# Folding the square sums of x on VectorE, and a new place for loads and fill work, in one layer of a gated encoder

## The chip, the cores and the metric

The kernel runs on one core of a Trainium2 chip. Five engines work side by side, each through its own list of instructions in order: TensorE (PE, with its weight loads as PEld), VectorE (DVE), ScalarE (ACT), GpSimd (POOL) and SyncE (SP), which issues all DMA transfers here. They wait for each other through semaphores. The metric is the device time of one launch in microseconds (us), the median of the runs shown. Everything is float32 in and out.

## What is computed

One encoder layer is applied to two requests, a prompt of 1024 tokens and a sample of 512, with the same weights. Cut to what matters:

```
def encoder_layer(x, mem, ...):
    h = rms_norm(x, ln_pre)
    z = h @ w_in                                  # 1024 -> 6400 columns
    (pool_in, pool_gate, q, k, v, attn_gate, xq, x_gate, merge_logits) = split(z)
    pool_out = multiscale_pool(pool_in, w_pool, pool_scale)
    q = apply_rope(rms_norm(q, q_norm));  k = apply_rope(rms_norm(k, k_norm))
    attn_out = self_attention(q, k, v)            # 8 heads of 64, 2 groups of k and v
    cross_out = cross_attention(xq, rms_norm(mem, ln_mem), w_mem_kv)   # 4 heads of 128, 256 memory tokens
    branches = (pool_out * silu(pool_gate), attn_out * silu(attn_gate), cross_out * silu(x_gate))
    gates = sigmoid(merge_logits + b_merge)
    merged = sum(gates[n] * (branches[n] @ w_branch[n]) for n in range(3))
    return x + rms_norm(merged @ w_out, ln_post)
```

`rms_norm` divides each token by the root of its mean square, so before h exists the squares of all 1024 features of a token must be summed.

## The kernel before

Every matrix product keeps float32 accuracy with three products of a cheaper type: each operand is split into a high and a low part (`split`, lines 171 to 173: ACT copies the high part, DVE subtracts it from the value for the low part), and `mm3` (line 139) issues high times high, high times low and low times high. Tiles hold 128 partitions by 512, 1024 or 2048 elements. Activations lie transposed, features on partitions and tokens along the row, in blocks of 512 tokens (`BLK`).

The program runs through these parts:

- `mem_phase` (line 655) projects the memory tokens of both requests: four chunks of keys (`mk`, 24 matmuls each), then four weight tiles of values (`mv`, 96 matmuls together). It also needs the mean squares of the memory tokens. It is given the generator `others` and steps it with `next(others, None)`.
- `others` is `long_h` (line 235): it loads the prompt's x as four tiles of 1 MB (`q[i][j]`, feature half i, token block j), sums the squares, scales x to h and forms the seven sums and differences that a fast 2x2 block multiplication needs (`put`, `difference`).
- Mean squares: `squares` (line 206) squares a 128x2048 tile on ACT and hands back its four pieces of 512. `mean_squares` (line 198) sums over the partitions on PE, by matmuls of each 128x128 piece with two columns of ones, 4 token tiles by as many pieces as it is given. ACT copies the result, `rstd_of` takes the power -0.5 on POOL, and `spread` (line 212) puts the row on all partitions: a diagonal on DVE, then one PE product with ones.
- `products` (line 313) multiplies h of the prompt with the weights, pair after pair, seven block products of 12 matmuls for each; `plain` (line 388) does it for the sample, 24 matmuls a weight tile. A generator of tails (`kv_tail`, `q_tail`, `pool_tail`) is stepped along.
- Then `stream` (line 807) runs a list of units: 64 of self attention of the prompt, 8 of cross attention, 32 of self attention of the sample, 4 of cross attention. Each unit has three steps, `scores`, `turn` (transposes of the probabilities on PE, split by ACT and DVE) and `values`; `turn` comes `LAG`=2 units behind `scores` and `values` another `VLAG`=2 behind. `weave` (line 108) counts the PE cost of these steps and after each of them adds steps of a generator `fill` until `SHARE` of that cost is used up. The fill is the rest of the sample's input products and then `branches(0)`, the branch projections of the prompt's first token block (`merge`, 288 matmuls).
- `block` (line 886) runs what is left: `branches` and `out_phase` block by block.

The order of each engine's list is then set by a scheduler from this order of emission, from the dependencies through tile buffers (`M` has 14 buffers of 2048, `HU` 8 of 512, `RAW` 3 weight tiles) and from priorities (`high_priority`). Each engine, SP too, takes its list strictly in order.

Of the kernel before, what the change touches and what calls it, by code (L numbers as in the profile page):

```python
# [19 lines left out]
D = 1024  # L20
KC = D // P
BLK = 512
# [39 lines left out]
def encoder_kernel(ctx: ExitStack, tc, wt, xs, xts, mt, cols, rows, rope, edge, ys):  # L62
# [64 lines left out]
    def chain(*gs):  # L127
        for g in gs:
            yield from g
# [75 lines left out]

    def squares(x):

        sq = M(F32)
        act.activation(sq[:], x, AF.Square, scale=D ** -0.5)
        return [sq[:, c * BLK:(c + 1) * BLK] for c in range(4)]  # L210

    def spread(r, out=None):

# [21 lines left out]
    def long_h(xt, h):  # L235

        h += [[None] * 4 for _ in range(7)]
        xv = xt.rearrange("p (k t) -> p k t", k=KC)
        q = [[M(F32) for _ in range(2)] for _ in range(2)]
        for j in range(2):  # L240
            for i in range(2):
                load(q[i][j][:].rearrange("p (c n) -> p c n", c=4), xv[:, i * 4:i * 4 + 4, j * BLK:(j + 1) * BLK])
                yield
        r, sp = S(16), []
        for j in range(2):
            rj = r[:, j * TT:(j + 1) * TT]
            mean_squares(squares(q[0][j][:]) + squares(q[1][j][:]), rj)
            rstd_of(rj)
            sp.append(spread(rj))
        b11, b12, b21, b22 = [[q[i][j][:, :D], q[i][j][:, D:]] for i in range(2) for j in range(2)]  # L250

        def scaled(i, j):
            for c in range(4):
                x = q[i][j][:, c * BLK:(c + 1) * BLK]
                v.scalar_tensor_tensor(x, x, colt[:, i * 4 + c:i * 4 + c + 1], sp[j], op0=ALU.mult, op1=ALU.mult)

        def put(k, x):
            for c in range(2):
                parts_of(h[k], 2 * c, x[c])

        def difference(out, a, b):
            for c in range(2):
                v.tensor_tensor(out[c], a[c], b[c], op=ALU.subtract)

        scaled(0, 0)
        put(0, b11)
        scaled(1, 0)
        put(1, b21)
        scaled(0, 1)
        scaled(1, 1)  # L270
        t3, t4 = (U(), U()), (U(), U())
        difference(t3, b22, b12)
        difference(b12, b12, b11)
        difference(b11, b22, b12)
        put(2, b11)
        put(3, b12)
        put(4, t3)
        put(5, b22)
        difference(t4, b21, b11)
        put(6, t4)  # L280
# [374 lines left out]
    def mem_phase(mkd, mvd, others):  # L655
# [7 lines left out]
        for i in range(4):  # L663
            x = raw[i // 2][:, i % 2 * D:(i % 2 + 1) * D]
            hi, lo = sb.tile([P, 1024], F32R, tag="kt", bufs=4, name=nm("mh")), U(F32R)
            for k in range(2):
                s = slice(k * BLK, (k + 1) * BLK)
                g = colt[:, 8 + 2 * i + k:9 + 2 * i + k]
                act.activation(hi[:, s], x[:, s], AF.Copy, scale=g)
                v.scalar_tensor_tensor(lo[:, s], x[:, s], g, hi[:, s].bitcast(F32), op0=ALU.mult, op1=ALU.subtract)  # L670
                mh.append(hi[:, s])
                ml.append(lo[:, s])
        yield
        m = list(zip(mh, ml))
        r, sp = S(16), HU()

        def rstd():
            mean_squares(squares(raw[0][:]) + squares(raw[1][:]), r[:, :TT])
            rstd_of(r[:, :TT])
            spread(r[:, :TT], sp[:])  # L680

        for c in range(4):
            b, w = B(), ws.pop(0) if ws else weights("mk", c)
            for k in range(KC):
                mm3(b[:], w(slice(k * P, (k + 1) * P)), m[k], k == 0, k == KC - 1)
            if c == 0:
                rstd()
            next(others, None)
            yield
            t, hi, lo = HU(), HU(F32R), HU(F32R)  # L690
            with tc.high_priority(EVAC):
                v.tensor_tensor(t[:], b[:], sp[:], op=ALU.mult)
                split(hi[:], lo[:], t[:])
            for g in range(2):
                for s, x in enumerate((hi, lo)):
                    o = s * D + c * NMEM
                    nc.sync.dma_start(mkd[g][:, o:o + NMEM], x[:, g * NMEM:(g + 1) * NMEM].bitcast(F32))
# [34 lines left out]
    def attention(b, sc, kt, vt, L):  # L732
# [4 lines left out]
        units = [(jp, hd, j) for jp in range(TT // 2) for hd in range(NH) for j in range(2)]  # L737
        state = {}

        def scores(i):  # L740
            jp, hd, j = units[i]
            g = hd // (NH // NG)
            if hd == 0 and j == 0:
                t = M()
                for x in range(2):
                    load(t[:, x * D:(x + 1) * D].bitcast(F32), qd[b * TT + jp * 2 + x][:])
                state["q", jp] = t
            q = state["q", jp][:, j * D + hd * P:j * D + (hd + 1) * P]
            a = A()
            for n in range(L // 512):  # L750
                ns = slice(n * 512, n * 512 + 512)
                mm(a[:, ns], q, kt[g][0][:, ns], start=True, stop=False)
                mm(a[:, ns], q, kt[g][1][:, ns], start=False, stop=True)
            mx, sm, rc = S(1), S(1), S(1)
            with tc.high_priority(PMAX):
                v.reduce_max(mx[:], a[:, :L], axis=AX.X, negate=True)  # L756
                p = U()
                act.activation(p[:, :L], a[:, :L], AF.Exp, bias=mx[:], accum_out=sm[:])  # L758
            v.reciprocal(rc[:], sm[:])  # L759
            pool.tensor_scalar(p[:, :L], p[:, :L], rc[:], 1.0, op0=ALU.mult, op1=ALU.mult)  # L760
            state[i] = p
# [40 lines left out]
                pool.tensor_tensor(ot[:, :256], ot[:, :256], gt[:, :256], op=ALU.mult)  # L802
                nc.sync.dma_start(out[c][:, cs], ot[:, :256])

        return [(scores, turn, values, i) for i in range(len(units))]

    def stream(units):
        n = len(units)
        for i in range(n + LAG + VLAG):
            for k, lag in enumerate((0, LAG, LAG + VLAG)):  # L810
                if 0 <= i - lag < n:
                    units[i - lag][k](units[i - lag][3])
                    yield

    def cross(b, sc, mkd, mvd):
# [2 lines left out]
        xqd, gd, out = sc["xq"], sc["x_gate"], sc["br2"]  # L818
        state = {}

        def scores(c):
            xf, xq = HU(), U(F32R)
            load(xf[:], xqd[c][:, bs])
            qh, ql = xq[:, 0:BLK], xq[:, BLK:2 * BLK]
# [2 lines left out]
            if c == 0:  # L827
                for k, src in (("mk", mkd), ("mv", mvd)):
                    t = M()
                    load(t[:].bitcast(F32), src[:])  # L830
                    state[k] = [t[:, i * D:(i + 1) * D] for i in range(2)]
            mk = state["mk"]
            a = A()
            ms_ = slice(c * NMEM, (c + 1) * NMEM)
            for t in range(TT):
# [36 lines left out]
        return [(scores, turn, values, c) for c in range(NXH)]  # L872

    def branch_parts(field, bs):
        t = from_scratch(field, bs)
# [139 lines left out]
    scs, kts, vts, pairs, bg, _, drained = group(0)  # L1015
    run(plain(pairs[0], hs, bg))
    merged = []
    fill = chain(drained(plain(pairs[1], hs, bg)), branches(0, sc, merged))
# [4 lines left out]
    run(fill)  # L1023
    run(block(1, 0, sc, False, merged))
    run(block(1, 1, sc, False))
    run(block(0, 0, scs, True))
# [1 line left out]

LAG, VLAG, SHARE, LOOK, WAIT = 2, 2, 0.9, 1, 6

AHEAD, EVAC, PMAX, PTURN, LATER = 120, 200, 150, 150, 200

# [89 lines left out]
```

## Time and profile before

| | us |
|---|---|
| median of 3 runs (1556.06 to 1563.41) | 1559.63 |
| the profiled execution, its own time | 1562.16 |
| its span on the core | 1559.9 |
| PE busy in the span | 1501.1 (96%) |
| DVE, ACT, POOL busy | 970.6 (62%), 711.3 (46%), 271.7 (17%) |

A window row of the profile gives, for a stretch of the span, each engine's busy time with its number of instructions, then the clock granted to TensorE (1.00 is full), the share of the DMA engines in use and GB/s. A timeline row gives start, duration, engine, line, operation, output and inputs by their names (buffer numbers left out), shape and count, and in brackets how long the engine had waited and for what. A chain row gives start, length and what stood on the chain of work that ended last.

### The profile page before, as it was taken

To read this page: it belongs to the slowest core of one execution; us is meant where nothing else is said; L and a number is where in the kernel's file an instruction comes from. 1 tells how busy PE (TensorE), PEld (TensorE's weight loads), DVE (VectorE), ACT (ScalarE), POOL (GpSimd) and SP (SyncE) were. 2 spreads that over 40 slices of the span, in tenths; PEclk is the share of its full clock that TensorE was granted. 3 is DMA by queue.
4 is the path that set the end of the run, shared out by engine and by line. 5 is a ranking of instruction groups with operands and counts; after the bars stand their busy time and mean duration, and the time that the engine had idled before them with its cause. 6 is when DMAs were issued, how large, how long until landed. Compare 5 with 4: busy or idle time off the path is not lost.

```text
span 1559.9 us, 19916 instructions
## 1 busy us (share of the span) xinstructions
PE 1501.1 (96%) x7408; PEld 1245.8 (80%) x7408; DVE 970.6 (62%) x1250; ACT 711.3 (46%) x1097; POOL 271.7 (17%) x286
## 2 busy tenths in 40 slices
PE   7979999999999999999999999999799889999998
PEld 5867888888888888887888888888586678888887
DVE  3278668574746765565666666666577674674764
ACT  3334435454433545443555555556445453333322
POOL 0000011110000000210222222223313350150141
PEclk8779999999999999999999999999899899999999
DMA  6421224333331443254232323225734564864942
GB/s 225 135 82 54 100 71 139 103 130 107 98 122 56 157 141 115 83 165 139 85 116 75 102 74 116 75 84 191 256 129 136 174 211 137 296 228 135 334 165 81
DMA packets 88176, 211.40 MB, mean 136 GB/s; under 512 B 9872, under 2 KB 19216, under 8 KB 87312
## 3 DMA queue, kind: packets, MB, share of 16 engines
q1 hardware_dynamic: 88080, 210.14, 40.3%
q8 instruction: 58, 0.95, 0.2%
q14 instruction: 38, 0.31, 0.1%
HBM read 155.57 MB, written 54.53 MB: 135 GB/s over the span
## 4 chain that ended last, share of the span: by engine, by line
PE 87%; issue 3%; DVE 3%; ACT 3%; DMA 2%; POOL 0%; SPq 0%; DVEq 0%; POOLq 0%; ACTq 0%
PE B L133 68%; PE A L133 14%; PE A L137 5%; DVE wlo L169 1%; ACT med L172 1%; PE B L137 1%; ACT whi L172 1%; ACT u L843 1%; DMA hu<-x_gate 0%; DVE med L169 0%; DMA hu<-merge 0%; ACT u L758 0%; DMA med<-q 0%; DMA hu<-xq 0%; DMA hu<-wt 0%
## 5 line engine op out<-in xcount | busy, mean ns | idle before, releaser
L133 PE MATMUL B<-med,whi 128*128 128x512 f32 x2776 | 874.7, 395 | 11.3 <-ACT med L172 10.6
L133 PEld LDWEIGHTS B<-med,whi 128*128 128x128 f32 x2776 | 516.7, 189 | 117.8 <-ACT med L172 12.5
L133 PE MATMUL B<-med,wlo 128*128 128x512 f32 x1388 | 546.6, 394 | 6.7 <-DVE wlo L169 6.7
L169 DVE TENSOR_TENSOR wlo<-raw,whi 128x1024 fp32r<-128x1024 f32 (+1 forms) x168 | 212.9, 1267 | 169.1 <-ACT whi L172 161.0
L133 PEld LDWEIGHTS B<-med,wlo 128*128 128x128 f32 x1388 | 263.0, 189 | 64.1 <-DVE wlo L169 8.2
L172 ACT ACTIVATE whi<-raw 128x1024 fp32r<-128x1024 f32 (+1 forms) x168 | 167.4, 996 | 305.3 <-PE B L133 191.6
L172 ACT ACTIVATE med<-A 128x1024 fp32r<-128x1024 f32 (+1 forms) x108 | 97.0, 898 | 143.4 <-PE A L137 143.0
L760 POOL TENSOR_SCALAR u<-u,s 128x1024 f32<-128x1024 f32 (+1 forms) x96 | 94.3, 982 | 339.1 <-DVE s L759 305.1
L169 DVE TENSOR_TENSOR med<-A,med 128x1024 fp32r<-128x1024 f32 (+1 forms) x109 | 115.5, 1060 | 49.0 <-ACT med L172 47.9
L192 POOL TENSOR_SCALAR s<-s 128x16 f32<-128x16 f32 (+3 forms) x17 | 5.3, 311 | 712.3 <-DVE s L551 330.0
L756 DVE TENSOR_REDUCE s<-A 128x1 f32<-128x1024 f32 (+1 forms) x96 | 100.0, 1041 | 38.8 <-PE A L133 25.7
L758 ACT ACTIVATE u<-A,s 128x1024 f32<-128x1024 f32 (+1 forms) x96 | 93.2, 971 | 47.5 <-DVE s L756 44.5
L137 PE MATMUL A<-ident,u 128*128 128x128 f32 x784 | 108.5, 276 | 4.9 <-DVE u L411 1.5
L137 PEld LDWEIGHTS A<-ident,u 128*128 128x128 f32 x784 | 92.1, 142 | 23.3 <-issue 9.4
L133 PE MATMUL A<-kt,med 128*128 128x512 f32 x320 | 94.7, 409 | 4.6 <-ACT u L758 1.9
L910 POOL TENSOR_TENSOR med<-med,hu 128x512 f32<-128x512 f32 x48 | 73.1, 1532 | 116.2 <-DVE hu L908 116.2
L133 PE MATMUL A<-whi,med 128*128 128x512 f32 (+1 forms) x320 | 92.4, 368 | 0.2 <-ACT hu L939 0.2
L172 ACT ACTIVATE whi<-sum 128x1024 fp32r<-128x1024 f32 x50 | 53.1, 1062 | 67.7 <-PE B L133 64.3
L133 PEld LDWEIGHTS A<-kt,med 128*128 128x128 f32 x320 | 55.1, 188 | 26.0 <-ACT u L758 14.2
L169 DVE TENSOR_TENSOR wlo<-sum,whi 128x1024 fp32r<-128x1024 f32 x50 | 61.1, 1222 | 23.6 <-ACT whi L172 22.7
L133 PE MATMUL B<-med,vt 128*128 128x256 f32 x512 | 75.1, 287 | 0.6 <-ACT med L172 0.6
L353 ACT ACTIVATE hu<-B 128x512 f32<-128x512 f32 x75 | 44.5, 593 | 60.6 <-PE B L133 56.4
(171 smaller groups left out, 1621.2 us busy)
## 6 DMA issues: line engine op xcount, KB each, us to landing
raw<-wt SPq DMA_DIRECT2D x168, 512.0 KB, 3.6
merge<-hu SPq DMA_DIRECT2D x72, 256.0 KB, 2.1
hu<-merge SPq DMA_DIRECT2D x72, 256.0 KB, 4.8
med<-br SPq DMA_DIRECT2D x36, 256.0 KB, 5.2
q<-hu SPq DMA_DIRECT2D x24, 256.0 KB, 2.9
br<-hu SPq DMA_DIRECT2D x24, 256.0 KB, 2.5
med<-q SPq DMA_DIRECT2D x12, 512.0 KB, 5.6
med<-xt_prompt SPq DMA_DIRECT2D x4, 1024.0 KB, 7.3
```

Source lines behind the costliest of these rows:

```text
L133: pe.matmul(out, l, r, **k)
L137: pe.transpose(out, x, i[:])
L169: v.tensor_tensor(out, x, hi.bitcast(F32), op=ALU.subtract)
L172: act.activation(hi, x, AF.Copy)
L192: pool.tensor_scalar(ss, ss, EPS, 1.0, op0=ALU.add, op1=ALU.mult)
L353: act.activation(kept[k][:, :n], b, AF.Copy)
L756: v.reduce_max(mx[:], a[:, :L], axis=AX.X, negate=True)
L758: act.activation(p[:, :L], a[:, :L], AF.Exp, bias=mx[:], accum_out=sm[:])
L760: pool.tensor_scalar(p[:, :L], p[:, :L], rc[:], 1.0, op0=ALU.mult, op1=ALU.mult)
L843: act.activation(p[:, ns], a[:, ns], AF.Exp, bias=mx[:, t:t + 1], accum_out=sm[:, t:t + 1])
L910: pool.tensor_tensor(at, at, sg[:], op=ALU.add)
```

## The change

Seven edits go together.

1. `squares` folds: after ACT's squaring of 128x2048 two additions on DVE (1024 wide, then 512 wide) leave one piece of 512 instead of four. `mean_squares` so gets 2 pieces instead of 8: 8 small matmuls instead of 32, three times in the kernel.
2. `long_h` issues all its loads at once and has yields between its later stages.
3. `mem_phase` steps `others` once ahead of its own first chunk, so the four x tiles are loaded ahead of the third weight tile; after the first chunk it doesn't step, after the others it does, so the statistics and the scaling of x stand between the memory's chunks.
4. `attention` and `cross` get a fourth step, `ahead`, two units in front of `scores`: the loads of q, and for cross attention of xq (with its split), mk and mv.
5. `stream` runs four steps with lags -2, 0, `LAG` and `LAG + VLAG`.
6. The fill holds the sample's input products alone; `branches(0)` runs after the stream, on its own.
7. `SHARE` goes from 0.9 to 0.66.

```
     def squares(x):
-        sq = M(F32)
+        sq, a = M(F32), HU()
         act.activation(sq[:], x, AF.Square, scale=D ** -0.5)
-        return [sq[:, c * BLK:(c + 1) * BLK] for c in range(4)]
+        v.tensor_tensor(sq[:, :D], sq[:, :D], sq[:, D:], op=ALU.add)
+        v.tensor_tensor(a[:], sq[:, :BLK], sq[:, BLK:D], op=ALU.add)
+        return a
...
     def long_h(xt, h):
         for j in range(2):
             for i in range(2):
                 load(q[i][j][:].rearrange("p (c n) -> p c n", c=4), xv[:, i * 4:i * 4 + 4, j * BLK:(j + 1) * BLK])
-                yield
+        yield
         for j in range(2):
             rj = r[:, j * TT:(j + 1) * TT]
-            mean_squares(squares(q[0][j][:]) + squares(q[1][j][:]), rj)
+            mean_squares([squares(q[i][j][:]) for i in range(2)], rj)
             rstd_of(rj)
             sp.append(spread(rj))
+            yield
...
         scaled(0, 0)
         put(0, b11)
+        yield
         scaled(1, 0)
         put(1, b21)
+        yield
         scaled(0, 1)
         scaled(1, 1)
+        yield
...
     def mem_phase(mkd, mvd, others):
+        next(others)
         yield
...
             if c == 0:
                 rstd()
-            next(others, None)
+            else:
+                next(others, None)
             yield
...
     def stream(units):
         n = len(units)
-        for i in range(n + LAG + VLAG):
-            for k, lag in enumerate((0, LAG, LAG + VLAG)):
+        for i in range(-2, n + LAG + VLAG):
+            for k, lag in enumerate((-2, 0, LAG, LAG + VLAG)):
                 if 0 <= i - lag < n:
-                    units[i - lag][k](units[i - lag][3])
+                    units[i - lag][k](units[i - lag][4])
                     yield
...
-    fill = chain(drained(plain(pairs[1], hs, bg)), branches(0, sc, merged))
+    fill = drained(plain(pairs[1], hs, bg))
...
     weave(stream(units), fill, SHARE)
     run(fill)
+    run(branches(0, sc, merged))
...
-LAG, VLAG, SHARE, LOOK, WAIT = 2, 2, 0.9, 1, 6
+LAG, VLAG, SHARE, LOOK, WAIT = 2, 2, 0.66, 1, 6
```

Three places in the engines' lists show what moves. First SP's list at the start of the program, before: `mt` is the memory, `xt_prompt` is x, `wt` the weights, and `mk` the stores of the first chunk's result.

```order
L146 DMA med_92<-mt 128x1024 x2
L146 DMA raw_257<-wt 128x1024
L146 DMA raw_299<-wt 128x1024
L146 DMA raw_342<-wt 128x1024
L146 DMA med_205<-xt_prompt 128x4x512
L146 DMA med_207<-xt_prompt 128x4x512
L146 DMA med_206<-xt_prompt 128x4x512
L697 DMA mk_87<-hu_211 128x256
```

The same place in the change:

```order
L146 DMA med_92<-mt 128x1024 x2
L146 DMA med_133<-xt_prompt 128x4x512
L146 DMA med_135<-xt_prompt 128x4x512
L146 DMA med_134<-xt_prompt 128x4x512
L146 DMA med_136<-xt_prompt 128x4x512
L146 DMA raw_268<-wt 128x1024
L146 DMA raw_335<-wt 128x1024
```

The four x tiles (the fourth stood behind the stores of the first chunk) now come ahead of the third weight tile.

Second, DVE's list around the statistics of x, before: `u<-ident` are the diagonals of the two `spread` calls, line 255 scales x, `wlo` are low parts of weights and `med<-med` low parts of h.

```order
L169 TENSOR_TENSOR wlo_564<-raw_561,whi_563 128x1024
L216 TENSOR_TENSOR u_413<-ident,s_372 128x512
L165 TENSOR_SCALAR gains<-gains 128x64
L255 SCALAR_TENSOR_TENSOR med_205<-med_205,colt,B_415 128x512 x2
L216 TENSOR_TENSOR u_457<-ident,s_372 128x512
L255 SCALAR_TENSOR_TENSOR med_205<-med_205,colt,B_415 128x512 x2
L169 TENSOR_TENSOR med_465<-med_205,med_465 128x2x512
L255 SCALAR_TENSOR_TENSOR med_207<-med_207,colt,B_415 128x512
```

In the change (`hu_299` and `hu_304` are second additions of the fold, `hu_324` and `hu_326` belong to the third chunk of the memory's keys, and `wlo_390` to its first weight tile of values):

```order
L218 TENSOR_TENSOR u_253<-ident,s_230 128x512
L211 TENSOR_TENSOR hu_299<-med_298 128x512
L211 TENSOR_TENSOR hu_304<-med_303 128x512
L258 SCALAR_TENSOR_TENSOR med_133<-med_133,colt,B_255 128x512 x4
L169 TENSOR_TENSOR med_369<-med_133,med_369 128x2x512
L258 SCALAR_TENSOR_TENSOR med_135<-med_135,colt,B_255 128x512
L169 TENSOR_TENSOR med_372<-med_133,med_372 128x2x512
L700 TENSOR_TENSOR hu_324<-B_267,hu_142 128x512
L169 TENSOR_TENSOR wlo_390<-raw_387,whi_389 128x1024
L169 TENSOR_TENSOR hu_326<-hu_324,hu_325 128x512
L218 TENSOR_TENSOR u_320<-ident,s_230 128x512
```

Scaling and splitting of x's first block stood behind all of the memory's keys and both diagonals; now it stands ahead of the third chunk's results and of the second diagonal.

Third, PE's list in the sample's cross attention, near the end of the stream, before: `A<-med,u` are scores, `ident` marks transposes, and `whi` and `wlo` are branch weights.

```order
L133 MATMUL A_10488<-med_10484,u_10480 128x256 x12
L137 MATMUL A_10516<-ident,u_10402 128x128 x4
L133 MATMUL B_10532<-med_10447,whi_10452 128x512 x2
L133 MATMUL B_10532<-med_10447,wlo_10453 128x512
L133 MATMUL B_10523<-med_10406,med_4613 128x256
L133 MATMUL B_10638<-med_10444,whi_10632 128x512 x2
L133 MATMUL B_10638<-med_10444,wlo_10633 128x512
```

In the change `whi` and `wlo` are input weights (`med_4493` is a part of the sample's h), and `B_10233` and `B_10256` are values of the cross attention:

```order
L133 MATMUL A_10159<-med_9929,u_10049 128x256 x12
L137 MATMUL A_10186<-ident,u_10070 128x128 x8
L133 MATMUL B_10154<-med_10035,med_4559 128x256
L133 MATMUL B_10233<-med_10151,med_9931 128x512 x6
L133 MATMUL B_10256<-med_10195,med_9931 128x512
L133 MATMUL B_10273<-med_4493,whi_10269 128x512 x2
L133 MATMUL B_10273<-med_4493,wlo_10270 128x512
```

The scores and transposes stand closer together with fewer other products between, and the 288 products of `branches(0)` follow in one row behind the stream.

More of the change, by code (lines that the diff above doesn't have):

```diff
@@ L206, in squares @@
     def squares(x):
-        sq = M(F32)
+        sq, a = M(F32), HU()
         act.activation(sq[:], x, AF.Square, scale=D ** -0.5)
-        return [sq[:, c * BLK:(c + 1) * BLK] for c in range(4)]
+        v.tensor_tensor(sq[:, :D], sq[:, :D], sq[:, D:], op=ALU.add)
+        v.tensor_tensor(a[:], sq[:, :BLK], sq[:, BLK:D], op=ALU.add)
+        return a
     def spread(r, out=None):
@@ L242, in long_h @@
                 load(q[i][j][:].rearrange("p (c n) -> p c n", c=4), xv[:, i * 4:i * 4 + 4, j * BLK:(j + 1) * BLK])
-                yield
+        yield
         r, sp = S(16), []
@@ L246, in long_h @@
             rj = r[:, j * TT:(j + 1) * TT]
-            mean_squares(squares(q[0][j][:]) + squares(q[1][j][:]), rj)
+            mean_squares([squares(q[i][j][:]) for i in range(2)], rj)
             rstd_of(rj)
             sp.append(spread(rj))
+            yield
         b11, b12, b21, b22 = [[q[i][j][:, :D], q[i][j][:, D:]] for i in range(2) for j in range(2)]
@@ L266, in long_h @@
         put(0, b11)
+        yield
         scaled(1, 0)
         put(1, b21)
+        yield
         scaled(0, 1)
         scaled(1, 1)
+        yield
         t3, t4 = (U(), U()), (U(), U())
@@ L672, in mem_phase @@
                 ml.append(lo[:, s])
+        next(others)
         yield
@@ L677, in rstd @@
         def rstd():
-            mean_squares(squares(raw[0][:]) + squares(raw[1][:]), r[:, :TT])
+            mean_squares([squares(raw[i][:]) for i in range(2)], r[:, :TT])
             rstd_of(r[:, :TT])
@@ L687, in mem_phase @@
                 rstd()
-            next(others, None)
+            else:
+                next(others, None)
             yield
@@ L738, in attention, with ahead @@
         state = {}
-        def scores(i):
+        def ahead(i):
             jp, hd, j = units[i]
-            g = hd // (NH // NG)
             if hd == 0 and j == 0:
@@ L747, in scores @@
                 state["q", jp] = t
+        def scores(i):
+            jp, hd, j = units[i]
+            g = hd // (NH // NG)
             q = state["q", jp][:, j * D + hd * P:j * D + (hd + 1) * P]
@@ L803, in values @@
                 nc.sync.dma_start(out[c][:, cs], ot[:, :256])
-        return [(scores, turn, values, i) for i in range(len(units))]
+        return [(ahead, scores, turn, values, i) for i in range(len(units))]
     def stream(units):
         n = len(units)
-        for i in range(n + LAG + VLAG):
-            for k, lag in enumerate((0, LAG, LAG + VLAG)):
+        for i in range(-2, n + LAG + VLAG):
+            for k, lag in enumerate((-2, 0, LAG, LAG + VLAG)):
                 if 0 <= i - lag < n:
-                    units[i - lag][k](units[i - lag][3])
+                    units[i - lag][k](units[i - lag][4])
                     yield
@@ L819, in cross, with ahead @@
         state = {}
-        def scores(c):
+        def ahead(c):
             xf, xq = HU(), U(F32R)
@@ L831, in scores @@
                     state[k] = [t[:, i * D:(i + 1) * D] for i in range(2)]
+            state["q", c] = qh, ql
+        def scores(c):
             mk = state["mk"]
+            qh, ql = state.pop(("q", c))
             a = A()
@@ L870, in values @@
             nc.sync.dma_start(out[c][:, bs], g[:])
-        return [(scores, turn, values, c) for c in range(NXH)]
+        return [(ahead, scores, turn, values, c) for c in range(NXH)]
     def branch_parts(field, bs):
@@ L1017, in encoder_kernel @@
     merged = []
-    fill = chain(drained(plain(pairs[1], hs, bg)), branches(0, sc, merged))
+    fill = drained(plain(pairs[1], hs, bg))
     units = [u for b in range(2) for u in attention(b, sc, kt, vt, 1024)]
@@ L1023, in encoder_kernel @@
     run(fill)
+    run(branches(0, sc, merged))
     run(block(1, 0, sc, False, merged))
@@ L1026, in encoder_kernel @@
     run(block(0, 0, scs, True))
[L1031 removed]
+LAG, VLAG, SHARE, LOOK, WAIT = 2, 2, 0.66, 1, 6
 AHEAD, EVAC, PMAX, PTURN, LATER = 120, 200, 150, 150, 200
```

## The prediction, made before the changed kernel ran

> **What bounds the kernel now.** I read the shares of the page first, then its slices, then the chain.
>
> ```profile
> span 1559.9 us, 19916 instructions
> PE 1501.1 (96%) x7408; PEld 1245.8 (80%) x7408; DVE 970.6 (62%) x1250; ACT 711.3 (46%) x1097; POOL 271.7 (17%) x286
> ...
> PE   7979999999999999999999999999799889999998
> ...
> PEclk8779999999999999999999999999899899999999
> ...
> PE 87%; issue 3%; DVE 3%; ACT 3%; DMA 2%; POOL 0%; SPq 0%; DVEq 0%; POOLq 0%; ACTq 0%
> ```
>
> PE is the bound nearly everywhere. Only slices with a low PE digit or a low clock have something to give: the first four and those around 1070 to 1290 us. Windows of both (PE busy, later its clock):
>
> ```profile
> 0.00:40.00 40.00, 28.78 (x122) 23.76 (x123) 12.98 (x20) 15.95 (x20) 1.92 (x8) 0.83 0.64 227
> 40.00:80.00 40.00, 40.00 (x194) 35.62 (x194) 9.73 (x13) 11.33 (x10) 1.21 (x2) 0.76 0.38 124
> ...
> 20.00:25.00 5.00, 5.00 (x26) 5.00 (x25) 0.00 (x0) 0.00 (x0) 0.00 (x0) 0.50 0.89 327
> ...
> 100.00:130.00 30.00, 18.49 (x57) 13.24 (x56) 29.69 (x33) 15.12 (x18) 0.00 (x0) 0.82 0.28 88
> ...
> 729.80:1063.50 333.70, 332.72 (x1916) 282.03 (x1917) 211.91 (x259) 192.43 (x277) 83.37 (x79) 1.00 0.30 98
> 1063.50:1130.70 67.20, 56.13 (x312) 47.26 (x311) 37.27 (x43) 35.94 (x91) 22.12 (x34) 0.90 0.63 211
> 1130.70:1235.00 104.30, 95.83 (x511) 75.27 (x509) 78.10 (x136) 55.82 (x117) 35.22 (x44) 1.00 0.42 131
> 1235.00:1289.20 54.20, 46.53 (x230) 37.87 (x231) 36.80 (x47) 25.20 (x56) 23.68 (x27) 0.91 0.67 232
> ```
>
> The last four are the stream: self attention of the prompt, its cross attention, self attention of the sample, its cross attention. The first loses nothing; the others lose 11.1, 8.5 and 7.7 us of PE and some clock. At the start the busy PE deceives: from 40 to 80 us it is 40.00 busy, yet at a clock of 0.76.
>
> **The start.** What fills PE there, and where the stage ends:
>
> ```profile
> 17.63 9.95 PE L133 MATMUL B<-ones,med 128*128 128x2 f32 x56
> 29.98 2.08 PE L133 MATMUL B<-u,ones 128*128 128x512 f32 x2 [2.40 <-DVE u L216]
> ...
> 54.65 10.97 PE L133 MATMUL B<-ones,med 128*128 128x2 f32 x64
> ...
> 71.85 11.09 PE L133 MATMUL B<-ones,med 128*128 128x2 f32 x64
> ...
> 106.51 0.80 PE L133 MATMUL B<-med,wlo 128*128 128x512 f32 x1 [5.32 <-DVE wlo L169]
> ...
> 139.86 0.97 PE L137 MATMUL A<-ident,u 128*128 128x128 f32 x7
> ```
>
> The ones-matmuls (two records each) cost 10.97 us for 32, 0.34 us apiece, at half clock. Behind them DVE becomes the bound: from 100 to 130 us it is busy 29.69 of 30 and PE 18.49. My milestone is the end of the first tail's eight transposes, 140.6 us (the last row above and its start-to-start); both programs have the same products ahead of it, except 72 ones-matmuls, and PE runs densely behind it.
>
> A rule of the Trainium skill speaks against edit 1 ("TensorE: Matmul & The Clock Gate", Part 1, on the 53.3 ns): start-to-start is at least about 25 ns however few columns, so the 144 records that go would be an estimated 3.6 us of PE, and folding them hardly worth its additions on DVE. The rows say 171 ns a record (10.97 us by 64), 24.6 us for 144. The Trainium skill's same page (Part 1, the two states) lets the clock fall after an idle window of some 3.4 us; the row of 20 to 25 us shows 0.50 with PE busy throughout, so by the trace tiny matmuls don't hold it up. The sum goes by the rows.
>
> Removing them makes DVE the bound of the start, so I price the new order there.
>
> ```profile
> 4.53 9.08 SPq L146 DMA_DIRECT2D raw<-wt  x3
> ...
> 36.18 0.45 SPq L146 DMA_DIRECT2D med<-xt_prompt  x1
> ...
> 11.43 1.89 ACT L209 ACTIVATE med<-med 128x2048 f32<-128x2048 f32 x1
> ...
> 28.16 1.03 POOL L196 TENSOR_TENSOR s<-s,mhalf 128x4 f32<-128x4 f32 x1
> ...
> 98.10 2.06 DVE L255 SCALAR_TENSOR_TENSOR med<-med,colt,B 128x512 f32<-128x512 f32 x3
> 111.16 4.63 DVE L263 TENSOR_TENSOR med<-med,med 128x1024 f32<-128x1024 f32 x4
> 147.41 0.68 DVE L328 TENSOR_TENSOR sum<-raw,raw 128x512 f32<-128x512 f32 x1
> 148.01 0.68 DVE L329 TENSOR_TENSOR sum<-raw,sum 128x512 f32<-128x512 f32 x1
> ```
>
> - Loads: SP stood 9.08 us on weights waiting for raw buffers and issued the fourth x tile at 36. Now x goes straight through. Memory, two weight tiles, x and the third weight tile are 7.9 MB; at the 327 GB/s of the row from 20 to 25 us that is 24 us. That weight's high part stands on ACT ahead of the copy of the memory's statistics: 24 + 1.1, then 1.03 on POOL with its small neighbours and one diagonal: the second chunk starts at about 29, against 31 (behind the 29.98 row). The delayed weights cost nothing here, being hidden by the wait for the statistics. If that cover goes, the third chunk starves, a few us.
> - DVE from about 26 us to the first pair's last low part, by its list: 32 operations of 1024 (4.63/4 = 1.16 us), 24 of 512 (0.60 start to start), 20 scalings and evacuations (2.06/3 = 0.69): 37 + 14.4 + 13.8 = 65 us, end at 91. Folding costs 6 x (1.16 + 0.60) = 10.6 us of DVE in all; 4.7 are in this sum, the rest lies where DVE idled. ACT's six squarings of 1.89 stay.
> - Waits of DVE for PE in that stretch (the second chunk's result, two `spread` chains, the copies of the first pair's products): I take 7.5 us, so 98.5, and 1.5 for PE's last products and transposes: **milestone at 100**, a gain of 40. Without any wait 93 (gain 47); with 11.2 us more of them, as much as PE stood idle from 0 to 80 (40 - 28.78), 111 (gain 29).
> - PE is no bound here: 276 matmuls by 0.227 are 63, 24 ones-matmuls by 0.34 are 8, and with the idle and half-clock stretches of the first 40 us (11.2, and 0.17 of 28.78) it could be done by about 87.
>
> **The stream.** The same products in total (1445 of 512 columns), elsewhere.
>
> ```profile
> 864.67 1.08 PE L133 MATMUL A<-kt,med 128*128 128x512 f32 x4
> ...
> 868.83 1.19 PE L133 MATMUL A<-kt,med 128*128 128x512 f32 x4
> ...
> 901.40 1.10 PE L133 MATMUL A<-kt,med 128*128 128x512 f32 x4
> ...
> 906.93 1.07 PE L133 MATMUL A<-kt,med 128*128 128x512 f32 x4
> ...
> 1028.85 1.20 PE L133 MATMUL A<-kt,med 128*128 128x512 f32 x4
> ...
> 1032.71 1.20 PE L133 MATMUL A<-kt,med 128*128 128x512 f32 x4
> ...
> 1311.14 2.72 PE B L133 x12
> ...
> PE B L133 <- ACT med L172: 10.4, 11, 4.3
> PE A L133 <- ACT u L825: 6.2, 4, 3.1
> PE A L133 <- DMA med<-mk: 2.6, 1, 2.6
> PE A L133 <- ACT u L758: 1.9, 4, 0.7
> ```
>
> - Self attention of the prompt: a unit with 12 fill matmuls takes 5.53 (906.93 - 901.40), of which 2.72 is fill, so 2.81 bare. One with 6 took 4.16 (2.81 + 1.36 = 4.17: no loss), one with 4 took 3.86 (3.72: 0.14 lost). The new order has 4 to 12, on average 8. 185 fill matmuls leave the stage, 42 us; at 0.1 us lost by 64 units it takes 333.7 - 42 + 6 = 298. They return behind the stream at 0.227 each, so the net is **+6**. Bounds: 0, and 64 x 0.3 = 19.
> - Cross attention of the prompt: waits (first three of the last rows, for 1060 to 1290 us) on xq's split and on mk, which `ahead` moves two units earlier, and on splits of branch inputs, which go away. Idle 11.1 and clock (1 - 0.90) x 56 = 5.6 make 16.7. Next is late the release of the score buffers by four exponentials; I leave 5: **-11.5**. Bounds: 0, -16.7. The loads moved are the same loads; on SP they now stand ahead of two units' stores and weight loads and hold one of 14 buffers that much longer. I cost this at nothing, hidden by the dense fill of the units before; without that cover it is the 2.6 of the mk row once more.
> - Self attention of the sample: idle 8.5. Little fill again, but the merge adds on POOL and its gate multiplications on DVE go: **-3**, bounds +5, -8.
> - Its cross attention: 7.7 and 0.09 x 46.5 = 4.2. Branch loads from scratch now queue on SP behind the last units' stores, so `branches(0)` can start a little late: **-6**, bounds +3, -12.
> - `branches(0)` alone: as dense as the second block's (12 matmuls in 2.72, above). Nothing.
>
> Stream: -14.5 (bounds +27, -37, not all at once; I carry +8 and -30).
>
> **Sum.** 1562.2 (the profiled execution's own time) - 40 - 14.5 = 1507.7; that execution lay 2.5 above the median of 1559.6, so 1505.
>
> **Rivals.**
> 1. Only the start gains: light units and the new queue behind the last stores eat the stream's gain (+8 in place of -14.5): 1527. For it: units of this trace already wait for exponentials (the 1.9 row). Against: the units of 4.16 and 3.86.
> 2. The start gains less: DVE's strict list puts memory results, the wait for spreads and x in one row, and the milestone lands at 115: 1520. For: 7.5 us of waits is my estimate. Against: ACT and PE have slack there.
> 3. Slower: the units keep their pace. If a unit is bound by its own chain (scores, maximum, exponential, release of two buffers) and not by PE, then the first three stages stay 333.7, 67.2 and 104.3 long and the 247 fill matmuls that leave them add 247 x 0.227 = 56 us behind: 1559.6 + 56 - 40 - 6 = 1570. It decides from the point where these stages shrink by under 10 us in all. Against: 3.86.
> 4. The change doesn't reach PE: x's loads take the bandwidth of the memory and of the weights, PE starves as long as it saved: 1545 (start gain 0). For: 64% of the DMA engines are in use already up to 40 us. Against: mem and two weights are issued ahead of x.
>
> **How the numbers follow.** Forecast, 1488 to 1518 around 1505: 0.66. Rival 1: 0.12; rival 2: 0.12, partly inside; rival 3: 0.04; rival 4: 0.03; better than 1488 (no waits of DVE): 0.03. The range goes from 47 + 28 gained (1485) to 29 gained and 0 from the stream (1531, rounded up): 1485 to 1532. A difference under 0.5% (8 us) can't be told from none here. Faster 0.94, same 0.02, slower 0.04.
>
> **What would show it.** Right: the eight transposes of the first tail end near 100 us, with DVE busy above 85% from 40 to 95; ones-matmuls in three groups of at most 2.8 us; units of self attention of 4.7 us on average; cross attention without waits on xq; one row of 288 branch matmuls in 66 us. Wrong: DVE idle in the start for over 15 us, PE waiting for `whi` of the third chunk, units that stay at 5.5 us, or gaps of several us between the last cross unit and the first branch product.

## The result, and the profile after

The changed kernel takes 1512.52 us, the median of 4 runs (1511.38 to 1514.27), against 1559.15 for the kernel before beside it: a ratio of 0.970, 95% interval 0.9675 to 0.9726. The profiled execution's own time is 1511.38, its span 1509.6. The forecast was 1505.

The page of the changed kernel, its shares, slices and chain:

```profile
span 1509.6 us, 19658 instructions
PE 1462.9 (97%) x7264; PEld 1207.9 (80%) x7264; DVE 981.2 (65%) x1262; ACT 709.2 (47%) x1097; POOL 272.4 (18%) x286
...
PE   5999999999999999999999999999989999999998
...
PEclk8999999999999999999999999999999999999999
...
PE 83%; issue 4%; ACT 4%; DVE 4%; DMA 2%; POOL 1%; SPq 0%; DVEq 0%; POOLq 0%; ACTq 0%
```

144 PE records are gone (7408 to 7264: 72 ones-matmuls of two records), and so are the low digits and low clocks around 1070 to 1290 us; only the first slice is still far below the others. Windows of the start, then of the stream's four stages (from the first score of each to that of the next; the last ends with the last transposes):

```profile
0.00:40.00 40.00, 21.91 (x82) 16.55 (x82) 22.89 (x31) 22.68 (x24) 2.90 (x9) 0.83 0.71 259
40.00:80.00 40.00, 37.50 (x154) 29.33 (x155) 35.55 (x45) 12.22 (x14) 2.50 (x4) 0.91 0.39 106
80.00:100.00 20.00, 18.86 (x82) 14.63 (x80) 19.46 (x21) 14.17 (x19) 0.00 (x0) 1.00 0.45 158
...
695.53:1000.02 304.49, 297.14 (x1729) 248.57 (x1729) 202.49 (x251) 177.95 (x261) 80.97 (x77) 0.99 0.28 90
1000.02:1046.68 46.66, 46.37 (x294) 40.65 (x294) 32.32 (x41) 31.96 (x88) 18.51 (x33) 1.00 0.60 197
1046.68:1141.17 94.49, 87.33 (x484) 68.74 (x482) 64.27 (x120) 57.45 (x122) 29.75 (x41) 1.00 0.41 136
1141.17:1163.62 22.45, 21.41 (x138) 18.25 (x137) 16.95 (x23) 17.48 (x48) 9.32 (x18) 1.00 0.54 173
```

From 40 us on two engines are nearly full, PE (the first busy column, 37.50 of 40 us and 18.86 of 20) and DVE (the third, 35.55 and 19.46). The prompt's cross attention has PE busy for 46.37 of 46.66 us. Timeline rows of PE in the start:

```profile
19.50 1.93 PE L133 MATMUL B<-ones,hu 128*128 128x2 f32 x14 [1.48 <-DVE hu L211]
...
28.56 2.08 PE L133 MATMUL B<-u,ones 128*128 128x512 f32 x2 [7.12 <-DVE u L218]
...
37.84 1.84 PE L133 MATMUL B<-ones,hu 128*128 128x2 f32 x16
...
51.50 1.84 PE L133 MATMUL B<-ones,hu 128*128 128x2 f32 x16
...
106.44 0.98 PE L137 MATMUL A<-ident,u 128*128 128x128 f32 x7
```

The milestone, the end of the first tail's transposes, falls from 140.6 to 107.4 us. The first score of the stream comes at 695.53 in place of 729.79, which is 34.3 us earlier.

The span is 50.3 us shorter. It divides at the stages' first scores. 185 fill matmuls left the first stage and 19 (by the two lists of PE) the second; at 0.227 us each they are credited there and debited behind.

| part | before | after | fill moved | net | predicted |
|---|---|---|---|---|---|
| up to the first score | 729.8 | 695.5 | | -34.3 | -40 |
| self attention of the prompt | 333.7 | 304.5 | +42.0 | +12.8 | +6 |
| its cross attention | 67.2 | 46.7 | +4.3 | -16.2 | -11.5 |
| all behind (both sample stages, branches, output) | 429.2 | 462.9 | -46.3 | -12.6 | -9 |

### The profile page after: what moved, and what is told of

It reads as the page before. It is cut to its first block, busy times and chain, and to the rows that moved or that the text cites. A ratio compares the mean times of both kernels' runs of the same rounds, so it can differ in the third digit from the quotient of the medians.

```text
span 1509.6 us, 19658 instructions
## 1 busy us (share of the span) xinstructions
PE 1462.9 (97%) x7264; PEld 1207.9 (80%) x7264; DVE 981.2 (65%) x1262; ACT 709.2 (47%) x1097; POOL 272.4 (18%) x286
## 4 chain that ended last, share of the span: by engine, by line
PE 83%; issue 4%; ACT 4%; DVE 4%; DMA 2%; POOL 1%; SPq 0%; DVEq 0%; POOLq 0%; ACTq 0%
PE B L133 65%; PE A L133 13%; PE A L137 5%; ACT u L769 1%; DMA hu<-xq 1%; DVE wlo L169 1%; ACT med L172 1%; ACT whi L172 1%; DVE s L767 1%; PE B L137 1%; DMA hu<-merge 1%; POOL med L925 1%; POOL s L196 0%; DVE med L169 0%; DMA med<-q 0%
## 5 line engine op out<-in xcount | busy, mean ns | idle before, releaser
L769 ACT ACTIVATE u<-A,s 128x1024 f32<-128x1024 f32 (+1 forms) x96 | 93.1, 970 | 46.3 <-DVE s L767 45.8
L925 POOL TENSOR_TENSOR med<-med,hu 128x512 f32<-128x512 f32 x48 | 77.4, 1625 | 136.1 <-DVE hu L923 136.1
L133 PEld LDWEIGHTS A<-kt,med 128*128 128x128 f32 x320 | 54.4, 190 | 34.2 <-ACT u L769 22.9
L169 DVE TENSOR_TENSOR med<-med,med 128x1024 fp32r<-128x1024 f32 (+1 forms) x50 | 55.5, 1115 | 33.7 <-ACT med L172 29.9
L172 ACT ACTIVATE med<-med 128x1024 fp32r<-128x1024 f32 (+1 forms) x44 | 44.3, 1019 | 68.8 <-POOL med L925 42.6
```

Of the source, the lines that this page charges most:

```text
L133: pe.matmul(out, l, r, **k)
L169: v.tensor_tensor(out, x, hi.bitcast(F32), op=ALU.subtract)
L172: act.activation(hi, x, AF.Copy)
L925: pool.tensor_tensor(at, at, sg[:], op=ALU.add)
```

## The experiments

Each kernel was timed beside the kernel before on the same chip, and the medians are compared within a call: 1559.94, 1559.25 and 1557.48 us for before in the three calls. First scores of profiles with the same start lie up to 3.3 us apart (726.45 to 729.79 with the old one), so smaller differences of one profile are not read.

### Start and stream apart

The first kernel has edits 1 to 3 alone, the second edits 4 to 7 alone.

> Edits 1 to 3 (fold, x's loads ahead, x's work between the memory's chunks) with the old stream. Theory: the gain is two parts that don't touch each other, about 34 us in the start and 18 in the stream. Then the first score of the stream starts at 695 us as in the whole change (before: 729.8), the stream stays 559 us long, and the time is about 1559 - 34 = 1525 (1521 to 1529). Rival (the parts need each other, because the tile buffers and the scheduler's order carry over): under 1518 or over 1533.

> Edits 4 to 7 (loads two units ahead, only input products as fill, share 0.66) with the old start. Theory of two separate parts: first score at 729.8 us as before, stream with the block behind it 16 to 18 us shorter, time about 1542 (1538 to 1546). Rival (the stream gains only because the start delivers something earlier): 1552 or more.

Measured: 1526.43 (-33.5; ratio 0.978, 0.977 to 0.980), first score 695.62; and 1544.82 (-15.1; 0.990, 0.987 to 0.993), first score 729.21. Together they give 48.6 us, against 46.6 for the whole: within the noise the two parts add up.

### The start taken apart

Edit 1 alone, and edits 2 and 3 alone. The cores of the two diffs:

```
     def squares(x):
...
-        return [sq[:, c * BLK:(c + 1) * BLK] for c in range(4)]
+        v.tensor_tensor(sq[:, :D], sq[:, :D], sq[:, D:], op=ALU.add)
+        v.tensor_tensor(a[:], sq[:, :BLK], sq[:, BLK:D], op=ALU.add)
+        return a
```

```
     def long_h(xt, h):
...
-                yield
+        yield
...
     def mem_phase(mkd, mvd, others):
...
+        next(others)
         yield
...
-            next(others, None)
+            else:
+                next(others, None)
```

> Edit 1 alone: 8 ones-matmuls in place of 32 per statistic, two additions on DVE per tile, the old order. Theory: three statistics stand one behind the other on the chain to DVE's work on x; each loses 24 x 0.34 = 8.2 us and gets 1.8 to 3.5 us of additions in their place, so the first score comes 14 to 19 us earlier (711 to 716) and the time is 1540 to 1545. Rival A (the fold is all of the start's gain): 30 us or more, under 1530. Rival B (the order is all of it; PE's matmuls were only filling its waits): under 5 us, over 1554.

> Edits 2 and 3 alone: x loaded ahead of the third weight tile and its statistics, scaling and splits between the memory's chunks, but with all 32 ones-matmuls per statistic. Theory: it gives what the fold doesn't, 34 - 16 = 18 us, 1541 (1536 to 1546), and the two add up. Rival A (the fold is all): over 1554. Rival B (the order is all): under 1530. Third case: each alone gives most of it, so the two overlap: this and the fold alone both under 1535.

Measured: the fold alone 1535.75 (-24.2), first score 704.75; the order alone 1545.07 (-14.9), first score 710.94. None of the cases fits whole. The order's time lies in its expected range, but the two don't add up: 25.0 + 18.9 at the first score is 9.7 more than the 34.2 of both (39.1 against 33.5 in time), so they overlap; where, no run here shows. The fold gave more than expected. PE rows of the kernel with the fold alone:

```profile
51.17 1.84 PE L133 MATMUL B<-ones,hu 128*128 128x2 f32 x16
...
56.82 1.84 PE L133 MATMUL B<-ones,hu 128*128 128x2 f32 x16
61.03 1.12 PE L133 MATMUL B<-u,ones 128*128 128x512 f32 x2 [0.64 <-DVE u L218]
```

The same spread in the kernel before:

```profile
86.36 1.91 PE L133 MATMUL B<-u,ones 128*128 128x512 f32 x2
```

x's second spread moved by 25.3 us, and the first score by 25.0. Two groups of 1.84 for two of 10.97 and 11.09 are 18.4 of it, the memory's spread (26.24 in place of 29.98) 3.7. The rest, some 3 us, fits the products behind each long group, which ran at half clock (0.63 us a record, against 0.39). My expectation had put 1.8 to 3.5 us of additions on the path for each statistic; for x they are hidden: neither of the two groups above waited for its sums.

The third question in the start is a wait on ACT. In the change the third weight tile lands behind x, and its high part stands in ACT's list ahead of the copy of the memory's statistics (the second row):

```profile
24.29 1.06 ACT L172 ACTIVATE whi<-raw 128x1024 fp32r<-128x1024 f32 x1 [3.29 <-DMA raw<-wt]
25.25 0.15 ACT L204 ACTIVATE s<-B 128x4 f32<-128x4 f32 x1
```

The experiment only swaps them, by taking the priority from this one tile's split:

```
-        with tc.high_priority(AHEAD):
+        with tc.high_priority(AHEAD if lead is None else lead):
             split(hi[:], lo[:], raw[:])
...
-            b, w = B(), ws.pop(0) if ws else weights("mk", c)
+            b, w = B(), ws.pop(0) if ws else weights("mk", c, lead=0 if c == 2 else None)
```

> The whole change, but the high and low part of the third weight tile are put into ACT's and DVE's lists behind the copy of the memory's statistics (no priority for this one tile). In the change ACT waited 3.29 us for that tile with the statistics' copy standing behind it. Theory: the delayed weight isn't hidden; without it ACT copies the statistics about 4 us earlier, the memory's spread comes at 24.5 in place of 28.56, all behind it moves by about as much, and the time is 1508 to 1509. Rival (what the prediction said: the wait for the statistics or DVE's own list hides it): first score within 1 us of 695.5, time 1511 to 1513.

ACT in this kernel, and below it PE's row of the memory's spread:

```profile
22.09 0.17 ACT L204 ACTIVATE s<-B 128x4 f32<-128x4 f32 x1 [1.08 <-PE B L133]
24.18 1.06 ACT L172 ACTIVATE whi<-raw 128x1024 fp32r<-128x1024 f32 x1 [1.92 <-DMA raw<-wt]
```

```profile
24.45 2.08 PE L133 MATMUL B<-u,ones 128*128 128x512 f32 x2 [2.40 <-DVE u L218]
```

The statistics are copied 3.2 us earlier, the spread comes at 24.45 in place of 28.56, and the first score at 691.02. In the two later kernels with the same swap it comes at 689.76 and 691.10; in the four with the change's start at 693.26 to 696.25. That is 4.5 us between the means. The time is 1507.04 (0.966, 0.963 to 0.969); its interval just overlaps that of the change (0.9675 to 0.9726), so the first scores are the better evidence. The theory held: the delayed weight was not hidden.

### The stream taken apart

Edits 4 and 5 alone, and edits 6 and 7 alone:

```
-        def scores(c):
+        def ahead(c):
...
-            for k, lag in enumerate((0, LAG, LAG + VLAG)):
+            for k, lag in enumerate((-2, 0, LAG, LAG + VLAG)):
```

```
-    fill = chain(drained(plain(pairs[1], hs, bg)), branches(0, sc, merged))
+    fill = drained(plain(pairs[1], hs, bg))
...
-LAG, VLAG, SHARE, LOOK, WAIT = 2, 2, 0.9, 1, 6
+LAG, VLAG, SHARE, LOOK, WAIT = 2, 2, 0.66, 1, 6
```

> Edits 4 and 5 alone on the kernel before: the loads of q, xq, mk and mv two units ahead; fill still the input products and then the branches of the first block, share 0.9. Theory: in the two cross-attention stages waits for xq's split and mk fall away (the mk row is 2.6 us, the longest split waits 4.3), the waits for splits of branch inputs stay: about 6 us less, 1553 (1550 to 1557), the self attention of the prompt stays at 333 us. Rival A (the loads ahead are all of the stream's 15 us): 1545. Rival B (they do nothing while the fill is what it was): 1559 to 1561.

> Edits 6 and 7 alone on the kernel before: only input products as fill, share 0.66, branches of the first block behind the stream; loads where they were. Theory: it gives the rest of the stream's 15 us, about 9, so 1550 (1546 to 1554): the branch work no longer mixes its splits, merge adds and loads into the short units, but xq and mk still come late (waits of 2 to 4 us in the cross stages stay). Rival A (the fill is all of it): 1545. Rival B (light units eat what the branches give back): 1558 or more.

Measured: the loads ahead alone 1543.54 (-15.7; 0.989, 0.986 to 0.992), the fill edits alone 1555.58 (-3.7; 0.998, 0.996 to 0.9998). Rival A of the first held: the loads ahead give as much as edits 4 to 7 together (-15.1), and with them in place the new fill adds nothing that can be measured. For the fill edits neither the theory (1546 to 1554) nor a rival fits; their 3.7 us are hardly more than noise: the profile of this kernel has the first score 3.3 us earlier than that of before, at 726.45, in a start that they don't touch. The prompt's cross attention with the loads ahead alone, in place of 67.20 us with PE busy 56.13:

```profile
1061.79:1112.99 51.20, 49.61 (x309) 43.42 (x309) 33.97 (x42) 34.49 (x89) 17.76 (x31) 1.00 0.60 205
```

It is nearly dense although branch work still fills it. So branch work in the fill was not by itself what made it wait. Which load it is, the next kernel asks: xq alone goes ahead, mk and mv stay in `scores`.

```
-        def scores(c):
+        def ahead(c):
             xf, xq = HU(), U(F32R)
             load(xf[:], xqd[c][:, bs])
...
+            state["q", c] = qh, ql
+
+        def scores(c):
             if c == 0:
                 for k, src in (("mk", mkd), ("mv", mvd)):
```

> On the kernel before, only cross attention's xq is loaded and split two units ahead; q, mk and mv stay where they were. Theory: of the 15.7 us of all loads ahead, the waits for xq's split are most (6.2 us in the row of waits, and behind them on ACT the splits of probabilities and branch inputs), the wait for mk is 2.6 to 4: 1547 (1544 to 1551). Rival (mk and mv at each stage's first unit are most of it): 1553 or more.

Measured: 1543.09 (-14.4; 0.990, 0.987 to 0.993), a little below the expected range. It can't be told from the -15.7 of all loads, so xq is nearly all of it. Three rows of the kernel before show such a load, on SP's queue, on ACT and on PE:

```profile
1072.11 1.40 SPq L146 DMA_DIRECT2D hu<-xq  x3
...
1076.78 0.63 ACT L825 ACTIVATE u<-hu 128x512 fp32r<-128x512 f32 x1 [1.01 <-DMA hu<-xq]
...
1077.46 0.50 PE L133 MATMUL A<-med,u 128*128 128x256 f32 x2 [0.48 <-ACT u L825]
```

The first of three loads is issued at 1072.11, its split follows 4.7 us later and the scores at once behind it. All of the unit's chain (scores, maximum, exponentials, transposes, split) starts that late. This is the only one of the twelve splits whose row has a wait for its load; the experiment moves load and split together, so it doesn't tell which of the two counts.

What the gain consists of can be read from PE between the first score and the end, first in the kernel before, then with xq ahead:

```profile
729.79:1559.90 830.11, 794.95 (x4213) 663.46 (x4213) 522.32 (x650) 396.61 (x664) 225.16 (x233) 0.98 0.45 152
```

```profile
729.54:1545.00 815.46, 789.04 (x4213) 660.46 (x4213) 519.52 (x650) 396.84 (x664) 221.26 (x233) 0.99 0.46 154
```

PE has as many instructions in both. It stands idle for 8.7 us less (35.2 and 26.4) and is busy for 5.9 us less. The 8.7 match the two rows of waits that go away, 6.2 for xq's split and 2.6 for mk (this one too, though mk's load stays in `scores`). The largest row of before, PE's waits for the splits of probabilities (10.4 us), is still there with xq ahead, from 1060 to 1290 us:

```profile
PE B L133 <- ACT med L172: 10.4, 11, 4.8
```

The 5.9 us are in no row of waits. They go with the clock, which in the prompt's cross attention was 0.90 before and is 0.97 with xq ahead.

Two kernels cover the fill within the whole change: one without edits 6 and 7 (their hunks above undone), and one without edit 7 alone:

```
-LAG, VLAG, SHARE, LOOK, WAIT = 2, 2, 0.66, 1, 6
+LAG, VLAG, SHARE, LOOK, WAIT = 2, 2, 0.9, 1, 6
```

> The whole change without edits 6 and 7: fold, order and loads ahead, with the fill and the share of before. Theory (after the runs of single parts): the stream's gain is the loads ahead, and moving the branches out of the fill adds nothing to it; start 33.5 and loads ahead 15.7 from 1559.2 make 1510 (1507 to 1514), against 1512.5 for the whole change. Rival (behind the new start the branches in the fill cost something): 1518 or more. Second rival (taking them out was a loss all along): under 1506.

> The whole change with edit 7 undone (share 0.9 in place of 0.66), so the input products run out about three quarters through the stream's units. Theory: a unit of the sample without fill loses 1.6 to 2.0 us and one of the prompt without fill well under 1; with some 30 such sample units and the cross units in front of them bare, 25 to 45 us are lost against the 12.6 + 2.9 lost now, and some 6 us come back in the prompt's self attention: 1525 to 1545. Rival (only the total of PE's work counts, where the fill lies doesn't): 1510 to 1515.

Without both: 1510.95 (0.970, 0.967 to 0.972), the same as the whole change. Without edit 7 alone: 1533.52 (0.983, 0.979 to 0.986), so edit 6 costs some 21 us unless edit 7 stretches the thinner fill. The sample's self attention of this kernel, and PE's waits from 1080 to 1190 us:

```profile
1080.62:1165.68 85.06, 61.71 (x334) 45.61 (x333) 58.83 (x117) 48.70 (x115) 28.26 (x42) 0.97 0.29 98
```

```profile
PE B L133 <- ACT med L172: 10.5, 16, 0.7
PE A L133 <- ACT u L769: 9.5, 24, 0.5
```

PE idles for 23.4 of 85 us there: bare units of the sample wait on their own chain, 24 times for an exponential and 16 times for a split in these 32 units and the four cross units behind them.

### Versions that might beat both

The first joins the best parts: fold, order, loads ahead, the old fill, and the swap on ACT (the diff with `lead` above). The second also sends fill to the sample:

```
+            if L == 512:
+                cost[0] += 700
...
-LAG, VLAG, SHARE, LOOK, WAIT = 2, 2, 0.9, 1, 6
+LAG, VLAG, SHARE, LOOK, WAIT = 2, 2, 0.8, 1, 6
```

> The kernel without edits 6 and 7, and the third weight tile's split behind the statistics' copy. Theory: that tile's place is worth 5.5 us in any stream (first score at 691, as in the whole change with it), so 1505 (1501 to 1508). Rival: under 2 us, first score at 695.

> The combined kernel with share 0.8, and 700 ns added to the counted cost of each of the sample's 32 self-attention units, which moves 76 fill matmuls out of the prompt's self attention (667 to 591) and 63 into the sample's (192 to 255). Theory: units of the prompt with 9 fill matmuls lose nothing, units of the sample with 0 to 3 lose 1.6 to 2.0 us; PE's idle time in the sample's self attention (11.5 us with 192) falls to about 6 and the time by 3 to 5 us against the combined kernel. Rival: the idle time there comes from the branches' own splits and merge adds, not from too little fill, and the time stays within 1 us or grows.

Measured: 1507.49 (0.967, 0.965 to 0.969) and 1508.34 (0.968, 0.966 to 0.971). The swap is worth its few us with the old fill too (1510.95 without it), but the new kernel can't be told from the change with the swap (1507.04). Sending fill to the sample gained nothing: PE's idle time in its self attention went from 12.0 to 10.9 us, not to 6, while the prompt's stage lost 2 us more. So the rival's number held, and too little fill is not the limit in that stage. Whether it is the branches' splits and merge adds, as the rival has it, remains open.

## Why the prediction was right, and where it was not

The time lies within the range and on the forecast side; 7.5 us separate it from 1505. Of these 3.7 are the sum (1507.7 predicted for the profiled execution, 1511.4 found) and 3.6 the last step: the profile of before was above its median, and I took the same for the one after, which lies 1.1 below its own. The four parts missed by more than their sum: by the table +5.7, +6.8, -4.7 and -3.6 us, which leaves 4.2. That the time came so near to 1505 is in part luck.

The range was also narrower than its own terms: its ends take 28 and 0 us for the stream, where the text carries -30 and +8. With these it would be 1483 to 1539.

**The start, -40 predicted, -34.3 found.** What was foreseen of DVE came about: it is above 85% busy from 40 us on, the ones-matmuls fell to groups of 2.3, 1.84 and 1.84 us, and no product waited for the third chunk's weights. DVE's sum was near as well: 66.0 us of work are done by 103 us, where the prediction had 65 done by 98.5. The mis-sized step is "PE is no bound here", done by about 87. From the second spread of x (55.84) to the milestone at 107.4, PE is as full as DVE:

```profile
28.56:55.84 27.28, 24.46 (x92) 18.36 (x93) 18.50 (x25) 7.29 (x11) 2.52 (x4) 0.77 0.27 81
55.84:107.43 51.59, 50.45 (x222) 40.12 (x223) 50.58 (x57) 25.71 (x30) 0.00 (x0) 1.00 0.38 118
```

All waits of PE up to 130 us, but for the one for its first weights:

```profile
PE B L133 <- DVE u L218: 9.9, 3, 7.1
...
PE B L133 <- DVE hu L211: 2.0, 2, 1.5
PE B L133 <- ACT hu L359: 1.1, 2, 1.0
```

PE waited for DVE only for the sums and diagonals of the statistics, up to 55.84; behind that its one row is 1.1 us for copies on ACT. The chain of work that ended last runs there on PE and, from 81 to 91 us, on ACT; from 25 us to the milestone DVE stands on it with three diagonals of 0.7 us alone. PE came to the milestone 20 us later than the 87 of the sum for two reasons. It stood idle for 21.7 us, not 11.2: it waited 7.1 us for the memory's spread, in place of 2.4, then 2.8 for the two of x, 2.0 for the folded sums and 1.1 for the copies. And it was busy for 85.7 us, not 76: the three spreads (5.2 us) and 15 transposes are not in the sum, and the low clock, which the sum had in the first 40 us only, is 0.77 from 28.56 to 55.84.

The sentence that the delayed weights "cost nothing here, being hidden by the wait for the statistics" was wrong too, though not in the sum, which had the second chunk at 29 with the weight ahead of the statistics' copy (it starts at 29.64). The fold makes the statistics ready at 21.4, so the weight was what came last. That wait cost 4.5 us at the first score; with the swap the first tail's transposes end at 103.3, in place of 107.4.

**The price of a ones-matmul.** 171 ns a record was right for what went, as a mean of two clocks; in the two groups of x that are left it is 115. The estimate that spoke against edit 1 took the least time from start to start, about 25 ns by the Trainium skill ("TensorE: Matmul & The Clock Gate", Part 1, on the 53.3 ns), as the price, which made 3.6 us of PE. The trace doesn't contradict the least, but it was not the price: these records took 100 ns even at full clock (the last section has the rows), and the fold alone measured 24.2 us.

**Self attention of the prompt, +6 predicted, +12.8 found.** Units average 4.76 us (304.49/64), near the 4.7 named, but the price of 0.1 us a unit was read from late units. Scores of the third to fifth unit after:

```profile
699.31 1.16 PE L133 MATMUL A<-kt,med 128*128 128x512 f32 x4
...
705.53 1.21 PE L133 MATMUL A<-kt,med 128*128 128x512 f32 x4 [1.84 <-ACT u L769]
...
712.27 1.78 PE L133 MATMUL A<-kt,med 128*128 128x512 f32 x4
```

And before:

```profile
733.55 1.18 PE L133 MATMUL A<-kt,med 128*128 128x512 f32 x4
...
739.79 1.20 PE L133 MATMUL A<-kt,med 128*128 128x512 f32 x4
```

The third unit takes 6.22 us with 7 fill matmuls, where it took 6.24 with 15. By the prediction's rule the third and fourth should take 4.40 and 3.95 us; they take 12.96 together, 4.6 too many. Here rival 3 is right on a small scale: the unit keeps the pace of its own chain. The row of 705.53 waited for an exponential, and ACT's rows ahead of it show why it was late:

```profile
701.93 1.06 ACT L172 ACTIVATE whi<-raw 128x1024 fp32r<-128x1024 f32 x1
702.90 0.58 ACT L464 ACTIVATE hu<-B 128x512 f32<-128x512 f32 x1
703.37 1.01 ACT L172 ACTIVATE med<-A 128x1024 fp32r<-128x1024 f32 x1
704.27 1.12 ACT L769 ACTIVATE u<-A,s 128x1024 f32<-128x1024 f32 x1
```

The exponential (the last row) stands without a gap behind a weight's high part, a copy of an input product and a copy of probabilities. Fifteen fill matmuls hid that, seven don't. The clock falls as well, to a mean of 0.60 between 705.53 and 712.27. Of the 12.8 us, 6.4 are more idle time of PE (7.35 us in the stage, 3.0 of it up to 720 us, against 1.0 before); the other 6.4 are busy time beyond what the moved fill explains, with a clock of 0.86 up to 720 us and 1.00 after it.

**Cross attention, -11.5 predicted, -16.2 found; all behind, -9 predicted, -12.6 found.** I left 5 us for the exponentials that release the score buffers; almost none are lost (46.37 busy of 46.66). Behind the stream the branch products run in one dense row, as forecast (from 1163.62 to 1230 us PE is busy all 66.38). In the rows of PE's waits from 690 to 1300 us neither xq nor mk is left:

```profile
PE A L133 <- ACT u L769: 8.8, 10, 1.8
PE A L137 <- DVE med L169: 2.1, 3, 1.5
PE B L133 <- ACT med L172: 1.6, 3, 1.1
```

**The reason for the stream's gain was half wrong.** The prediction credited it to the loads ahead and to the branch splits and merge adds that go away. The runs give all of it to edits 4 and 5, 14.4 of 15.7 us to xq; the fill edits move work from stage to stage (+12.8 in one, less in others) and end at nothing measurable once the loads are early. The sum came out because the net was right, not the shares.

**The rivals.** The first (the stream gains nothing) falls with edits 4 to 7 alone at -15.1. The second (milestone at 115) came half true, at 107.4: DVE idled longer than assumed (11.0 us from 26 to 103 us, against 7.5), 5.2 us of it for the memory's products, and what was said against it, that PE has slack there, was wrong. The third and fourth fall, but for the units above.

## What to carry to other kernels

Where an engine takes its list in order, ask of each instruction that waits for a load what stands behind it: one weight split ahead of a copy of 0.15 us cost 4.5 us, so that the first group of ones-matmuls became 7.6 us shorter and the spread behind it came only 1.4 us earlier; and the loads and splits of twelve short tiles at their use cost 14. The row of waits under the load's own name gives the idle time, but not the clock that falls with it: 8.8 us of waits went away and the run became 14.4 shorter. And when filler work is thinned out, price the units by the first ones as well as the steady ones.

## What the runs showed of the hardware that was not expected

Back-to-back matmuls of two columns do not hold the clock up. The prediction had read this from one row; windows show the fall itself, inside one group of 64 records in the kernel with the order alone (PE's busy time comes first, the granted clock third from the end: 1.00 to 0.50):

```profile
59.91:62.00 2.09, 2.09 (x21) 2.09 (x19) 1.68 (x2) 1.06 (x1) 0.00 (x0) 1.00 0.00 0
62.00:64.30 2.30, 2.30 (x23) 2.30 (x22) 0.24 (x1) 0.00 (x0) 0.00 (x0) 1.00 0.00 0
64.30:66.50 2.20, 2.20 (x17) 2.20 (x16) 0.00 (x0) 0.00 (x0) 0.00 (x0) 0.71 0.00 0
66.50:68.70 2.20, 2.20 (x12) 2.20 (x11) 0.00 (x0) 0.00 (x0) 0.00 (x0) 0.50 0.00 0
```

A record takes 100 ns (2.09 by 21) at full clock and 183 at half, and the clock falls between 4.4 and 6.6 us into the group. In the changed kernel, a group and what follows it:

```profile
37.84:39.70 1.86, 1.84 (x17) 1.75 (x15) 1.44 (x2) 1.06 (x1) 0.00 (x0) 1.00 0.00 0
39.70:42.20 2.50, 0.00 (x1) 0.03 (x1) 2.01 (x4) 0.69 (x2) 1.26 (x2) 0.83 0.32 104
42.20:47.90 5.70, 5.70 (x12) 3.80 (x13) 4.67 (x7) 1.93 (x2) 0.00 (x0) 0.50 0.58 141
```

The pause is 2.5 us, but with the 1.84 us of tiny matmuls ahead of it the clock falls all the same (0.83 in the pause, 0.50 behind it). The Trainium skill ("TensorE: Matmul & The Clock Gate", Part 1) lets the clock fall after an idle window of about 3.4 us; by that rule a pause of 2.5 us alone should mostly be safe. The trace agrees if such matmuls count as idle, and the group above, where the clock falls with no pause at all, fits that. What the clock goes by, no run here shows.
